# An encoder layer on one Trainium2 core: plain units behind each change of norm, with the new forms made in two stages, and half of the output projection without the seven-product scheme

## The chip, the cores and the metric

The kernel runs on one core of one Trainium2 chip. The metric is the device time of one execution in microseconds (us). Engines are named as in the profile: PE (TensorE, matrix products), DVE (VectorE), ACT (ScalarE), POOL (GpSimd) and SP (SyncE, which here only issues loads). Each engine works through its own queue in program order.

## The reference

One layer of a bidirectional encoder on 256 tokens (T = 256) of width D = 2048, in fp32:

```python
h = h + 1/2 * SwiGLU_1(RMSNorm(h))            # d_ff 5632
u = RMSNorm(h); z = u @ W_in                  # NA q|k|v, MLA q-latent, kv-latent, rope key, gate_A, gate_B
A  = NeighbourhoodAttention2D(q, k, v) @ W_branch_A
Bm = MLA(q-latent, kv-latent, rope key) @ W_branch_B
h = h + (sigmoid(gate_A) * A + sigmoid(gate_B) * Bm) @ W_out
h = h + 1/2 * SwiGLU_2(RMSNorm(h))
h = h + sigmoid(RMSNorm(h) @ W_pl_gate) * (p @ W_pl)
out = RMSNorm(h)
```

The norm is taken four times over the residual stream `h`. Three times matrix products follow at once: ahead of `W_in` (called "mix" in the code), ahead of the second feed-forward ("ffn2"), and ahead of `W_pl_gate` ("pl"). These are the three changes of norm.

## The kernel before

**Products.** An fp32 operand is held as two parts: `hi`, a cast on ACT (L90), and `lo`, a subtraction on DVE (L91). A product of two operands takes three matmuls, `hi*lo`, `hi*hi` and `lo*hi` (L95, L96, L97; `triple`). Weights come from HBM in raw pieces R, of which three are held, and are converted into W pieces by one ACT cast and one DVE subtraction each. An activation operand in this hi/lo layout, transposed so that features lie on partitions, is called a *form*. It covers 256 features (two chunks `kt` of 128); eight forms, 0 to 7, cover `h`. They are written into places X, H or O.

**Units and Blocks.** A `Unit` multiplies by 512 columns of a weight. It consists of granules (class `Granule`); one granule is two chunks of K, one load of 512 KB, one cast, one subtraction of 128x1024, and 12 matmuls for both halves of the tokens, in two PSUM banks. With K = 2048 a unit has 8 granules, 96 matmuls. A `Block` takes 1024 columns jointly over the same K. Of its eight chunk pairs, numbers 2, 4 and 6 (`SEVEN`) are done with 7 products of 2x2 blocks in place of 8; they come in two steps, SevenA and SevenB (9 and 12 matmuls). The other five are `Plain` steps (24 matmuls). So a Block takes 183 matmuls where two units take 192. It needs, of weights and of activations, sums of blocks: a weight chunk takes the DVE operations L259, L261, L262 and two L91 beside it, and its form holds eight tiles, four as they are and four sums. A unit needs the first four only. A Block uses all eight PSUM banks; at its end DVE puts the eight results together, L192 to L195 in `early` and L201 to L204 in the first half of `late`, and then `done` is called.

**Order.** The program is one list of steps (`grans`), in the order in which units and Blocks are made. At each step the next weights are converted ahead (`convert`), as many as there are free W pieces: a granule takes one of four, a Block's step two of six. Then the step's matmuls are issued, and then what `at(d, fn)` has put down for this step. At the last step of a Block (`e.end`) it is otherwise: its matmuls come first, with L192 to L195 and L201 to L204, and only then the next conversions and the rest of `done`.

**Changes of norm.** The last two Blocks ahead of a norm each end in `added`: four residual adds into `h` (L535), and then `new_forms` one and two steps later, which transposes the new columns of `h` on PE (L372), scales them by the norm's gain (L390, L393, L403) and, for forms 2, 4 and 6, builds the four sums (L362) in one scratch piece Z before all eight tiles are split (L90, L91). The squares for the norm follow at five and six steps (L468). The factor `rstd` is not in the forms; it is applied to the products. Behind ffn1 the next thing is the Block of the two latents, behind `W_out` the first Block of ffn2, behind ffn2 the Block of two quarters of `W_pl_gate`. Only ahead of the first feed-forward are there two plain units with forms made in two stages (`first_form`: four tiles; `more_form`: the sums).

**Between.** In the mixing part the latents' Block is followed by one unit of q (NA), the rope key (`kr`: 64 columns, one granule with all 16 chunks), the `W_ukv` and `W_uq` units, three more units of NA q and k; beside these and the Blocks of v the attention runs in small steps put down with `at`. Then come the branches, the gates, and `W_out` as two Blocks.

Of the kernel before, what the change touches and what calls it, by code (L numbers as in the profile page):

```python
# [27 lines left out]
def encoder_kernel(ctx, tc, x, p, ffn1_norm, ffn1_w_gate, ffn1_w_up, ffn1_w_down, mix_norm, w_in,  # L28
# [24 lines left out]
    MPLACE = [("X4", 0), ("X4", 1), ("X6", 0), ("H1", 0), ("X7", 0), ("H1", 1), ("H2", 0), ("H4", 0)]  # L53
    APART = ["H2", "W4", "W5", "H3"]

    def piece(tag, shape, dt=F32):
# [43 lines left out]
    class Unit:  # L100
        def __init__(self, src, K, N, xop, evac, by_token=False, xtile=None):
            self.src, self.K, self.N, self.xop, self.evac, self.by_token = src, K, N, xop, evac, by_token
            self.xtile = xtile or (lambda kt, t: tuple(a[:, t * P:t * P + P] for a in xop(kt)))
            self.per = 1024 // N
            self.load = 2 * self.per if N == 512 else self.per
            self.raw = self.ps = None
            self.kept = []
            self.early = not grans
            if self.early:
                self.load = 2  # L110
            for k0 in range(0, K, self.per):
                grans.append(Granule(self, k0, min(self.per, K - k0)))
# [275 lines left out]
    def scaled(o, ps, gc):  # L388
        if gc is None:
            S.copy(o, ps)  # L390
            return
        for k in range(2):
            S.activation(o[:, k * T:k * T + T], ps[:, k * T:k * T + T], AF.Copy, scale=gT[:, gc + k:gc + k + 1])  # L393
# [31 lines left out]
        at(1, flush)  # L425
        return f

    def new_forms(n, gname, full):
        for i in sorted((2 * n, 2 * n + 1), key=lambda i: i in SEVEN):
            forms[i] = make_form(XPLACE, i, i, h_tile, gcol[gname] + 2 * i, full)  # L430

    zs = []

    def first_form(i):
        ps = plain_tiles(h_tile, i)
        f = forms[i] = place(XPLACE, i)
        if i not in SEVEN:
            plain_form(f, ps, 2 * i)
            return
        if not zs:  # L440
            zs.append(piece("Z", [P, 4, 4, P]))
        z = zs[0][:, i // 2]
        scaled(z.rearrange("p a b -> p (a b)"), ps, 2 * i)
        split(f[:, 0, 0:4], f[:, 1, 0:4], z)

    def more_form(i):
        e = tmp.tile([P, 4, P], F32, tag="pt", name=nm("e"))
        sums(zs[0][:, i // 2], e)
        at(1, lambda: split(forms[i][:, 0, 4:8], forms[i][:, 1, 4:8], e))

    def first_tile(kt, t):
        f = forms[kt // 2]
        n = ((1, 0), (2, 3))[kt % 2][t]
        return f[:, 0, n, :], f[:, 1, n, :]

# [70 lines left out]
    def tmps(tag):  # L526
        return [tmp.tile([P, 512], F32, tag=tag, name=nm(tag)) for _ in range(2)]

    def added(n, nxt, full=True):

        def done(c11, c12, c21, c22):
            for k, t, o in ((n, 0, c11), (n, 1, c21), (n + 1, 0, c12), (n + 1, 1, c22)):
                hs = h[:, t, k * 512:k * 512 + 512]
                if nxt:
                    V.tensor_tensor(out=hs, in0=hs, in1=o, op=ALU.add)  # L535
                else:
                    G.dma_start(hs, o, accum_op=ALU.add)  # L537
            if nxt:
                for k in range(2):
                    at(1 + k, lambda k=k: new_forms(n + k, nxt, full))  # L540
                    next_stat(nxt, n + k, 5 + k)
        return done


# [55 lines left out]
    def mixer():  # L600
# [40 lines left out]
            V.tensor_tensor(out=dst[:, :, 32:64], in0=dst[:, :, 32:64], in1=w2, op=ALU.add)  # L641

        def kr_evac(ps):
            krT = tmp.tile([64, T], F32, tag="s", name=nm("krT"))
            V.tensor_copy(krT, ps[0][0:64, 0:T])

            def tr1():
                r = rstd["mix"]
                b = bank()
                for t in range(2):  # L650
                    PE.transpose(b[:, t * 64:t * 64 + 64], krT[:, t * P:t * P + P], ident[0:64, 0:64])
                kr = []
                for t in range(2):
                    z = tmp.tile([P, 1, 64], F32, tag="s", name=nm("krz"))
                    V.tensor_scalar(out=z[:, 0, :], in0=b[:, t * 64:t * 64 + 64], scalar1=r[:, t:t + 1], scalar2=None,
                                    op0=ALU.mult)
                    o = tmp.tile([P, 2, 64], F32, tag="pt", name=nm("kro"))
                    w = small([P, 2, 32], tag="krw")
                    rope(o[:, 0:1, :], z, t, 1, w[:, 0:1, :], w[:, 1:2, :])
                    V.tensor_copy(o[:, 1, :], o[:, 0, :])  # L660
                    kr.append(o)

                def tr2():
                    hold()
# [29 lines left out]
        def uq_evac(u):  # L694
            def f(ps):
# [5 lines left out]
                if u == 2:  # L701
# [93 lines left out]
        def mla_attention(d0):  # L795
# [28 lines left out]
            for pair in range(4):  # L824
                run(pair, d0 + 4 * pair)

            at(d0 + 17, loose)

        def na_qk_evac(which, u, place):
            def f(ps):  # L830
# [29 lines left out]
        def na_attention(d0):  # L860
# [21 lines left out]
            at(d0 + 17, end)  # L882

            def run(pair, d):
                holder = {}
# [19 lines left out]
                def rest():  # L905
                    B, C = pv_steps(heads, holder, lambda hd, kt: M["nv"][:, kt, hd * P:hd * P + P], None, True)
                    B()
                    at(1, C)
                at(d + 3, rest)
            for pair in range(4):  # L910
                run(pair, d0 + 4 * pair)

# [40 lines left out]
        def ya_evac(n):  # L953
            def f(ps):
                a = tmps("t")
                for t in range(2):
                    V.tensor_tensor(out=a[t], in0=ps[t], in1=M["sga", n, t], op=ALU.mult)
                for t in range(2):
                    V.tensor_tensor(out=a[t], in0=a[t], in1=M["yb"][t][:, n * 512:n * 512 + 512], op=ALU.add)

                def tr():
                    for j in sorted((0, 1), key=lambda j: 2 * n + j in SEVEN):
                        mixed[2 * n + j] = make_form(MPLACE, 2 * n + j, j, lambda t, kt: a[t][:, kt * P:kt * P + P],
                                                     scratch="X0")
                at(1, tr)
            return f

        def oop(key):
            def f(kt):
                o = M[key]  # L970
                return o[0][:, kt, :], o[1][:, kt, :]
            return f

        wi = w_in[0]
# [5 lines left out]
        def plain(c0, evac):  # L980
            unit(rows(wi, c0), 16, 512, None, evac, xtile=first_tile)

        joint(wi, 3584, 3072, x, latents)
        plain(0, na_qk_evac("nq", 0, "H1"))
        unit(rows(wi, 4096, 64), 16, 64, narrow_x, kr_evac)
        for u in range(4):
            unit(rows(w_ukv[0], u * 512), 4, 512, lop("kva"), ukv_evac(u))
# [12 lines left out]
            joint(wi, 4160 + n * 512, 4160 + n * 512 + 512, x, ga_done(n))  # L1000
        for n in range(4):
            unit(rows(w_branch_a[0], n * 512), 8, 512, oop("oa"), ya_evac(n))
        for n in (0, 2):
            joint(w_out[0], n * 512, n * 512 + 512, form_of(mixed), added(n, "ffn2", False))


    def embedding():
# [34 lines left out]
        def pl_evac(n):  # L1042
            def f(ps):
# [13 lines left out]
                def gain():  # L1057
                    for t in range(2):
                        gained(n, t)
                    if n == 2:  # L1060
# [64 lines left out]
    first_pl = len(grans)  # L1125
    E = embedding()
    tasks.setdefault(first_pl, []).append(E["start"])
    tasks.setdefault(first_pl + 1, []).append(lambda: at(1, E["ptr"]))
# [110 lines left out]
```

## Time and profile before

| | |
|---|---|
| runs | 2180.14, 2182.2, 2182.46 us; median 2182.2 us |
| the profiled execution | 2180.34 us, of which the span of the profile is 2178.6 us |
| matmuls and transposes on PE | 9621 |
| busy: PE, DVE, ACT, POOL | 2132.2, 1857.8, 1175.9, 46.5 us |
| HBM | 409.83 MB read, 189 GB/s over the span |

How to read it: times are us from the start of the span. A line of instructions names the engine, the line of the code and `out<-in` in the program's names, with the shape in partitions x elements. In square brackets stands the idle time ahead of an instruction and what ended it. In windows, the columns are the length, the busy time of the engine (with its instructions), the granted clock of PE as a share of full speed, the busy share of the DMA engines and their GB/s.

### The profile page before, as it was taken

To read this page: it belongs to the slowest core of one execution; us is meant where nothing else is said; L and a number is where in the kernel's file an instruction comes from. 1 tells how busy PE (TensorE), PEld (TensorE's weight loads), DVE (VectorE), ACT (ScalarE), POOL (GpSimd) and SP (SyncE) were. 2 spreads that over 40 slices of the span, in tenths; PEclk is the share of its full clock that TensorE was granted. 3 is DMA by queue.
4 is the path that set the end of the run, shared out by engine and by line. 5 is a ranking of instruction groups with operands and counts; after the bars stand their busy time and mean duration, and the time that the engine had idled before them with its cause. 6 is when DMAs were issued, how large, how long until landed. Compare 5 with 4: busy or idle time off the path is not lost.

```text
span 2178.6 us, 25574 instructions
## 1 busy us (share of the span) xinstructions
PE 2132.2 (98%) x9621; PEld 1762.7 (81%) x9621; DVE 1857.8 (85%) x2005; ACT 1175.9 (54%) x1178; POOL 46.5 (2%) x70
## 2 busy tenths in 40 slices
PE   9999999999999899999999999899999999999987
PEld 8888888888887688888888887788888888888766
DVE  6899889998999875576688789899989998899986
ACT  7455455555556545454555555555555555555554
POOL 1000100000000000001000000000000000000000
PEclk9999999999999999999999999999999999999999
DMA  7555866667665455356556555566676657756643
GB/s 261 185 193 195 242 204 207 198 213 220 202 207 176 148 175 172 119 195 193 170 176 210 189 191 163 171 203 202 213 217 207 207 189 226 232 175 202 208 155 135
DMA packets 219052, 422.00 MB, mean 194 GB/s; under 512 B 14600, under 2 KB 15184, under 8 KB 218800
## 3 DMA queue, kind: packets, MB, share of 16 engines
q1 hardware_dynamic: 213072, 408.47, 56.7%
q0 software_dynamic: 5824, 11.89, 3.1%
q8 instruction: 75, 1.23, 0.2%
q14 instruction: 49, 0.40, 0.0%
q10 hardware_dynamic: 32, 0.01, 0.0%
HBM read 409.83 MB, written 2.10 MB: 189 GB/s over the span
## 4 chain that ended last, share of the span: by engine, by line
PE 91%; DVE 4%; ACT 2%; issue 2%; DMA 1%; DVEq 0%; ACTq 0%; POOL 0%; POOLq 0%
PE B L97 29%; PE B L95 29%; PE B L96 29%; DVE W L91 2%; PE B L372 2%; ACT W L90 1%; DMA R<-in_w_branch_b_dram 1%; PE B L783 1%; PE B L769 0%; PE B L811 0%; PE B L810 0%; DVE X L91 0%; ACT sq L468 0%; PE B L894 0%; ACT Z L393 0%
## 5 line engine op out<-in xcount | busy, mean ns | idle before, releaser
L90 ACT CAST W<-R 128x1024 fp32r<-128x1024 f32 (+2 forms) x681 | 936.8, 1382 | 674.3 <-DVE R L259 365.3
L91 DVE TENSOR_TENSOR W<-R,W 128x1024 fp32r<-128x1024 f32 (+2 forms) x681 | 1094.5, 1629 | 211.9 <-ACT W L90 210.3
L95 PE MATMUL B<-W,X 128*128 128x512 f32 x2019 | 796.8, 395 | 16.9 <-DVE H L337 7.6
L97 PE MATMUL B<-W,X 128*128 128x512 f32 x2019 | 789.8, 391 | 6.5 <-DVE W L91 6.5
L96 PE MATMUL B<-W,X 128*128 128x512 f32 x2019 | 788.2, 390 | 0.0
L95 PEld LDWEIGHTS B<-W,X 128*128 128x128 f32 x2019 | 380.8, 189 | 98.7 <-DVE H L337 8.0
L97 PEld LDWEIGHTS B<-W,X 128*128 128x128 f32 x2019 | 380.6, 189 | 88.9 <-DVE W L91 9.1
L96 PEld LDWEIGHTS B<-W,X 128*128 128x128 f32 x2019 | 381.0, 189 | 77.5
L97 PE MATMUL B<-W,H 128*128 128x512 f32 x934 | 364.5, 390 | 6.0 <-DVE W L91 5.7
L95 PE MATMUL B<-W,H 128*128 128x512 f32 x934 | 366.2, 392 | 0.0
L96 PE MATMUL B<-W,H 128*128 128x512 f32 x934 | 363.5, 389 | 0.0
L97 PEld LDWEIGHTS B<-W,H 128*128 128x128 f32 x934 | 175.3, 188 | 45.4 <-DVE W L91 9.0
L96 PEld LDWEIGHTS B<-W,H 128*128 128x128 f32 x934 | 175.4, 188 | 36.0
L95 PEld LDWEIGHTS B<-W,H 128*128 128x128 f32 x934 | 175.4, 188 | 35.7
L259 DVE TENSOR_TENSOR R<-R 128x1024 f32<-128x1024 f32 x119 | 145.8, 1225 | 4.1
L262 DVE TENSOR_TENSOR R<-R 128x512 f32<-128x512 f32 x119 | 82.4, 693 | 4.0
L261 DVE TENSOR_TENSOR R<-R 128x512 f32<-128x512 f32 x119 | 82.4, 692 | 4.1
L390 ACT CAST H<-B 128x512 fp32r<-128x512 f32 x31 | 17.7, 588 | 96.9 <-PE B L372 96.9
L562 ACT ACTIVATE s<-t,sm 128x512 f32<-128x512 f32 x42 | 28.1, 716 | 30.1 <-DVE t L201 30.1
L537 POOL DMA_DIRECT2D h<-t x16 | 13.9, 998 | 1361.8 <-DVE t L201 1143.1
L393 ACT ACTIVATE X<-B,gT 128x256 fp32r<-128x256 f32 x40 | 16.5, 472 | 36.2 <-PE B L372 36.2
L193 DVE TENSOR_TENSOR t<-B,pt 128x512 f32<-128x512 f32 x41 | 28.4, 692 | 1.4
(229 smaller groups left out, 974.4 us busy)
## 6 DMA issues: line engine op xcount, KB each, us to landing
R<-in_ffn_w_down_dram SPq DMA_DIRECT2D x176, 512.0 KB, 5.2
R<-in_ffn_w_gate_dram SPq DMA_DIRECT2D x170, 512.0 KB, 3.8
R<-in_ffn_w_up_dram SPq DMA_DIRECT2D x168, 512.0 KB, 4.8
R<-in_w_in_dram SPq DMA_DIRECT2D x81, 512.0 KB, 4.6
R<-in_w_in_dram SPq DMA_DIRECT2D x24, 1024.0 KB, 5.2
R<-in_w_out_dram SPq DMA_DIRECT2D x32, 512.0 KB, 5.0
R<-in_w_branch_b_dram SPq DMA_DIRECT2D x8, 1024.0 KB, 7.1
R<-in_w_branch_a_dram SPq DMA_DIRECT2D x8, 1024.0 KB, 5.0
```

Of the source, the lines that this page charges most:

```text
L90: S.copy(hi, r)
L91: V.tensor_tensor(out=lo, in0=r, in1=hi.bitcast(F32), op=ALU.subtract)
L95: PE.matmul(o, xl, hi, start=start, stop=False)
L96: PE.matmul(o, xh, hi, start=False, stop=False)
L97: PE.matmul(o, xh, lo, start=False, stop=stop)
L193: V.tensor_tensor(out=self.v, in0=q[7], in1=self.w, op=ALU.add)
L259: V.tensor_tensor(out=raw[:, 0:4:3, :], in0=raw[:, 0:3:2, :], in1=raw[:, 3:4, :].to_broadcast([P, 2, 512]), op=ALU.add)
L261: V.tensor_tensor(out=raw[:, 2, :], in0=raw[:, 0, :], in1=raw[:, 2, :], op=ALU.add)
L262: V.tensor_tensor(out=raw[:, 1, :], in0=raw[:, 2, :], in1=raw[:, 1, :], op=ALU.add)
L372: PE.transpose(ps[:, j * P:j * P + P], src(t, 2 * i + k), ident)
L562: S.activation(s[t], g, AF.Silu, scale=r[:, t:t + 1])
L783: PE.matmul(b[:, j * T:j * T + T], vsl(heads[j], kt), pts[j][:, kt, :], start=(kt == 0), stop=(kt == 1))
```

## The change

It has these parts.

1. **Plain units behind the norms.** Behind ffn1 the first unit of NA q now stands ahead of the latents' Block. Behind ffn2 one unit of `W_pl_gate` and its `W_pl` unit stand ahead of the gates' Block. The second half of `W_out` is two plain units; the first half stays a Block.
2. **Forms in two stages.** For "mix" and "pl", `added` now makes four tiles per form one and two steps later (`first_form`), and the sums of forms 2, 4 and 6 at four, six and eight steps (`more_form`). The scratch Z holds all three forms' tiles at once. The squares move to (4, 7) steps behind the first down Block and (3, 5) behind the second.
3. **W_out.** The Block ends in `wout_done` (residual, forms at +1 and +2, squares at +3 and +4). A plain unit ends in `wout_evac`: the two residual adds read PSUM themselves, and `new_forms` follows at +1.
4. **At a Block's end** the first granule of a unit that follows is now converted ahead of the Block's last matmuls, L192 to L195 and L201 to L204 (`convert(True)`).
5. **Smaller parts.** `kr` is two granules with loads of half the size. One step of the NA attention (`rest`) comes a step later, and the steps that depend on counts are shifted by one. `MPLACE` (the places of the forms of `W_out`) has other entries. The tasks of the last part are counted and placed anew.

```diff
-            self.per = 1024 // N
+            self.per = min(1024 // N, 8)
...
+    def first_form(i, gc=0):
         ps = plain_tiles(h_tile, i)
         f = forms[i] = place(XPLACE, i)
         if i not in SEVEN:
-            plain_form(f, ps, 2 * i)
+            plain_form(f, ps, gc + 2 * i)
             return
-        if not zs:
+        if len(zs) % 3 == 0:
             zs.append(piece("Z", [P, 4, 4, P]))
-        z = zs[0][:, i // 2]
-        scaled(z.rearrange("p a b -> p (a b)"), ps, 2 * i)
+        else:
+            zs.append(zs[-1])
+        z = zs[-1][:, i // 2]
+        scaled(z.rearrange("p a b -> p (a b)"), ps, gc + 2 * i)
         split(f[:, 0, 0:4], f[:, 1, 0:4], z)
...
-            if nxt:
-                for k in range(2):
-                    at(1 + k, lambda k=k: new_forms(n + k, nxt, full))
-                    next_stat(nxt, n + k, 5 + k)
+            for k in range(2):
+                for j in range(2):
+                    at(1 + k, lambda i=2 * (n + k) + j: first_form(i, gcol[nxt]))
+                next_stat(nxt, n + k, (4, 7)[k] if n == 0 else 3 + 2 * k)
+            if n == 2:
+                for j, i in enumerate(sorted(SEVEN)):
+                    at(4 + 2 * j, lambda i=i: more_form(i))
...
-                at(d + 3, rest)
+                at(d + 4, rest)
...
+        def wout_done(*c):
+            for k, t, o in four(0, *c):
+                residual(k, t, o)
+            for k in range(2):
+                at(1 + k, lambda k=k: new_forms(k, "ffn2"))
+                next_stat("ffn2", k, 3 + k)
+
+        def wout_evac(n):
+            def f(ps):
+                for t in range(2):
+                    residual(n, t, ps[t])
+                at(1, lambda: new_forms(n, "ffn2"))
+                next_stat("ffn2", n, 2 if n == 2 else 4)
+            return f
...
+        plain(0, na_qk_evac("nq", 0, "H1"))
         joint(wi, 3584, 3072, x, latents)
-        plain(0, na_qk_evac("nq", 0, "H1"))
...
-        for n in (0, 2):
-            joint(w_out[0], n * 512, n * 512 + 512, form_of(mixed), added(n, "ffn2", False))
+        joint(w_out[0], 0, 512, form_of(mixed), wout_done)
+        for n in (2, 3):
+            unit(rows(w_out[0], n * 512), 16, 512, None, wout_evac(n), xtile=lambda kt, t: plain_tile(mixed, kt, t))
...
+        unit(rows(wg, 1024), 16, 512, None, gate_evac(2), xtile=first_tile)
+        unit(rows(wp, 1024), 2, 512, pop, pl_evac(2))
         Block([rows(wg, 0), rows(wg, 512)], form_of(forms), 8, gates)
-        unit(rows(wp, 0), 2, 512, pop, pl_evac(0))
-        unit(rows(wp, 512), 2, 512, pop, pl_evac(1))
-        unit(rows(wg, 1024), 16, 512, None, gate_evac(2), xtile=first_tile)
+        for n in range(2):
+            unit(rows(wp, n * 512), 2, 512, pop, pl_evac(n))
         unit(rows(wp, 1536), 2, 512, pop, last_pl_evac)
-        unit(rows(wp, 1024), 2, 512, pop, pl_evac(2))
         unit(rows(wg, 1536), 16, 512, None, last_gate_evac, by_token=True, xtile=first_tile)
...
-    def convert():
+    def convert(one=False):
...
-            if step[0] < 0:
+            if one or step[0] < 0:
                 return
...
+        elif ends and todo[0] < len(grans) and isinstance(grans[todo[0]], Granule):
+            convert(True)
```

Three places in the order of DVE show what moves. The names: W are weight pieces (the L91 writes `lo`), R raw pieces, B PSUM banks, t and pt the results of a Block, h the residual stream, X forms, Z the scratch.

The first place is DVE behind the last four L20x of ffn1's last Block, before:

```order
L91 TENSOR_TENSOR W_816_5379<-R_814_5375,W_815_5378 128x2048
L535 TENSOR_TENSOR h<-h,t_5362 128x512
L535 TENSOR_TENSOR h<-h,t_5363 128x512
L535 TENSOR_TENSOR h<-h,pt_5364 128x512
L535 TENSOR_TENSOR h<-h,pt_5365 128x512
L91 TENSOR_TENSOR W_819_5390<-R_817_5386,W_818_5389 128x1536
L259 TENSOR_TENSOR R_817_5386<-R_817_5386 128x2x512
L261 TENSOR_TENSOR R_817_5386<-R_817_5386 128x512
L262 TENSOR_TENSOR R_817_5386<-R_817_5386 128x512
L403 SCALAR_TENSOR_TENSOR X_782_5202<-B_824_5424,gT,X_782_5202 128x256 x2
L362 TENSOR_TENSOR Z_5439<-Z_5439 128x128 x4
L91 TENSOR_TENSOR W_829_5447<-R_817_5386,W_828_5446 128x2x512
```

The same place with the change:

```order
L537 TENSOR_TENSOR h<-h,t_5359 128x512
L537 TENSOR_TENSOR h<-h,t_5360 128x512
L537 TENSOR_TENSOR h<-h,pt_5361 128x512
L537 TENSOR_TENSOR h<-h,pt_5362 128x512
L91 TENSOR_TENSOR W_815_5378<-R_814_5376,W_815_5378 128x1024
L91 TENSOR_TENSOR W_816_5381<-R_814_5376,W_816_5381 128x1024
L91 TENSOR_TENSOR X_820_5403<-Z_5203,X_820_5403 128x512
L403 SCALAR_TENSOR_TENSOR X_785_5213<-B_821_5408,gT,X_785_5213 128x256 x2
L91 TENSOR_TENSOR W_823_5419<-R_822_5417,W_823_5419 128x1024
L91 TENSOR_TENSOR X_825_5439<-Z_5203,X_825_5439 128x512
L403 SCALAR_TENSOR_TENSOR X_827_5449<-B_826_5444,gT,X_827_5449 128x256 x2
L91 TENSOR_TENSOR W_828_5454<-R_822_5417,W_828_5454 128x1024
```

The residual adds stand ahead of the next conversions, these are single granules in place of Block steps with their sums, and the splits of forms have half the elements.

The second place is DVE at the end of the last Block of ffn2. Before:

```order
L91 TENSOR_TENSOR W_2380_15133<-R_2378_15129,W_2379_15132 128x2048
L91 TENSOR_TENSOR W_2385_15153<-R_2383_15149,W_2384_15152 128x2048
L192 TENSOR_TENSOR pt_15194<-B_2371_15090,t_15192 128x512
L193 TENSOR_TENSOR t_15193<-B_2370_15083,pt_15194 128x512
L194 TENSOR_TENSOR pt_15195<-B_2369_15079,t_15193 128x512
L195 TENSOR_TENSOR pt_15194<-B_2369_15079,pt_15194 128x512
L201 TENSOR_TENSOR t_15192<-B_2348_14950,t_15192 128x512
L202 TENSOR_TENSOR t_15193<-B_2349_14957,t_15193 128x512
L203 TENSOR_TENSOR pt_15195<-B_2350_14964,pt_15195 128x512
L204 TENSOR_TENSOR pt_15194<-B_2351_14971,pt_15194 128x512
L91 TENSOR_TENSOR W_2392_15209<-R_2390_15205,W_2391_15208 128x2048
L535 TENSOR_TENSOR h<-h,t_15192 128x512
```

With the change:

```order
L91 TENSOR_TENSOR W_2371_15128<-R_2370_15126,W_2371_15128 128x1024
L91 TENSOR_TENSOR W_2372_15131<-R_2370_15126,W_2372_15131 128x1024
L91 TENSOR_TENSOR W_2376_15152<-R_2375_15150,W_2376_15152 128x1024
L192 TENSOR_TENSOR pt_15181<-B_2360_15071,t_15179 128x512
L193 TENSOR_TENSOR t_15180<-B_2359_15064,pt_15181 128x512
L194 TENSOR_TENSOR pt_15182<-B_2358_15060,t_15180 128x512
L195 TENSOR_TENSOR pt_15181<-B_2358_15060,pt_15181 128x512
L201 TENSOR_TENSOR t_15179<-B_2337_14935,t_15179 128x512
L202 TENSOR_TENSOR t_15180<-B_2338_14942,t_15180 128x512
L203 TENSOR_TENSOR pt_15182<-B_2339_14949,pt_15182 128x512
L204 TENSOR_TENSOR pt_15181<-B_2340_14956,pt_15181 128x512
L91 TENSOR_TENSOR W_2381_15192<-R_2375_15150,W_2381_15192 128x1024
```

Three conversions of granules stand ahead of L192, and a fourth between L204 and the residual adds, which follow it.

The third place is DVE where the last Block of gate_A ends and the units of `W_branch_A` begin. Before:

```order
L91 TENSOR_TENSOR W_1421_8947<-R_1419_8943,W_1420_8946 128x2048
L192 TENSOR_TENSOR pt_8997<-B_1408_8841,t_8995 128x512
L193 TENSOR_TENSOR t_8996<-B_1407_8834,pt_8997 128x512
L194 TENSOR_TENSOR pt_8998<-B_1406_8830,t_8996 128x512
L195 TENSOR_TENSOR pt_8997<-B_1406_8830,pt_8997 128x512
L201 TENSOR_TENSOR t_8995<-B_1393_8745,t_8995 128x512
L202 TENSOR_TENSOR t_8996<-B_1394_8752,t_8996 128x512
L203 TENSOR_TENSOR pt_8998<-B_1395_8759,pt_8998 128x512
L204 TENSOR_TENSOR pt_8997<-B_1396_8766,pt_8997 128x512
L91 TENSOR_TENSOR W_1427_9010<-R_1426_9008,W_1427_9010 128x1024
L91 TENSOR_TENSOR W_1428_9013<-R_1426_9008,W_1428_9013 128x1024
```

With the change:

```order
L91 TENSOR_TENSOR W_1424_8959<-R_1422_8955,W_1423_8958 128x2048
L91 TENSOR_TENSOR W_1426_8985<-R_1425_8983,W_1426_8985 128x1024
L192 TENSOR_TENSOR pt_9014<-B_1411_8853,t_9012 128x512
L193 TENSOR_TENSOR t_9013<-B_1410_8846,pt_9014 128x512
L194 TENSOR_TENSOR pt_9015<-B_1409_8842,t_9013 128x512
L195 TENSOR_TENSOR pt_9014<-B_1409_8842,pt_9014 128x512
L201 TENSOR_TENSOR t_9012<-B_1396_8757,t_9012 128x512
L202 TENSOR_TENSOR t_9013<-B_1397_8764,t_9013 128x512
L203 TENSOR_TENSOR pt_9015<-B_1398_8771,pt_9015 128x512
L204 TENSOR_TENSOR pt_9014<-B_1399_8778,pt_9014 128x512
L91 TENSOR_TENSOR W_1431_9025<-R_1425_8983,W_1431_9025 128x1024
```

The first granule of the unit (`W_1426`) is converted ahead of L192 instead of behind L204.

More of the change, by code (lines that the diff above doesn't have):

```diff
@@ L51, in encoder_kernel @@
     HPLACE = [("H0", 0), ("H0", 1), ("H1", 0), ("H4", 0), ("H2", 0), ("H4", 1), ("H3", 0), ("H5", 0)]
-    MPLACE = [("X4", 0), ("X4", 1), ("X6", 0), ("H1", 0), ("X7", 0), ("H1", 1), ("H2", 0), ("H4", 0)]
+    MPLACE = [("X6", 0), ("X6", 1), ("H2", 0), ("H1", 0), ("X7", 0), ("H1", 1), ("H3", 0), ("H4", 0)]
     APART = ["H2", "W4", "W5", "H3"]
@@ L426, in make_form, with new_forms @@
         return f
-    def new_forms(n, gname, full):
+    def new_forms(n, gname):
         for i in sorted((2 * n, 2 * n + 1), key=lambda i: i in SEVEN):
-            forms[i] = make_form(XPLACE, i, i, h_tile, gcol[gname] + 2 * i, full)
+            forms[i] = make_form(XPLACE, i, i, h_tile, gcol[gname] + 2 * i)
     zs = []
-    def first_form(i):
+    def first_form(i, gc=0):
         ps = plain_tiles(h_tile, i)
@@ L447, in more_form, with plain_tile @@
         e = tmp.tile([P, 4, P], F32, tag="pt", name=nm("e"))
-        sums(zs[0][:, i // 2], e)
+        sums(zs[-1][:, i // 2], e)
         at(1, lambda: split(forms[i][:, 0, 4:8], forms[i][:, 1, 4:8], e))
     def first_tile(kt, t):
-        f = forms[kt // 2]
+        return plain_tile(forms, kt, t)
+    def plain_tile(table, kt, t):
+        f = table[kt // 2]
         n = ((1, 0), (2, 3))[kt % 2][t]
@@ L527, in tmps, with residual, added @@
         return [tmp.tile([P, 512], F32, tag=tag, name=nm(tag)) for _ in range(2)]
-    def added(n, nxt, full=True):
+    def residual(k, t, o):
+        hs = h[:, t, k * 512:k * 512 + 512]
+        V.tensor_tensor(out=hs, in0=hs, in1=o, op=ALU.add)
+    def added(n, nxt):
         def done(c11, c12, c21, c22):
             for k, t, o in ((n, 0, c11), (n, 1, c21), (n + 1, 0, c12), (n + 1, 1, c22)):
-                hs = h[:, t, k * 512:k * 512 + 512]
                 if nxt:
-                    V.tensor_tensor(out=hs, in0=hs, in1=o, op=ALU.add)
+                    residual(k, t, o)
                 else:
+                    hs = h[:, t, k * 512:k * 512 + 512]
                     G.dma_start(hs, o, accum_op=ALU.add)
-            if nxt:
-                for k in range(2):
-                    at(1 + k, lambda k=k: new_forms(n + k, nxt, full))
-                    next_stat(nxt, n + k, 5 + k)
+            if not nxt:
+                return
+            for k in range(2):
[5 more added lines that the diff above has]
+                    at(4 + 2 * j, lambda i=i: more_form(i))
         return done
@@ L643, in kr_evac @@
         def kr_evac(ps):
-            krT = tmp.tile([64, T], F32, tag="s", name=nm("krT"))
+            krT = tmp.tile([64, T], F32, tag="t", name=nm("krT"))
             V.tensor_copy(krT, ps[0][0:64, 0:T])
@@ L734, in f @@
                     at(4, rt)
-                    mla_attention(6)
+                    mla_attention(5)
             return f
@@ L825, in mla_attention @@
                 run(pair, d0 + 4 * pair)
-            at(d0 + 17, loose)
+            at(d0 + 18, loose)
         def na_qk_evac(which, u, place):
@@ L881, in end @@
                 split(*M["oa"], M["nq"])
-            at(d0 + 17, end)
+            at(d0 + 18, end)
             def run(pair, d):
@@ L963, in tr @@
                         mixed[2 * n + j] = make_form(MPLACE, 2 * n + j, j, lambda t, kt: a[t][:, kt * P:kt * P + P],
-                                                     scratch="X0")
+                                                     full=True, scratch="X0")
                 at(1, tr)
@@ L972, in oop @@
             return f
+        def wout_done(*c):
+            for k, t, o in four(0, *c):
+                residual(k, t, o)
+            for k in range(2):
[8 more added lines that the diff above has]
+            return f
         wi = w_in[0]
@@ L1059, in gain @@
                         gained(n, t)
-                    if n == 2:
+                    E["n"] = E.get("n", 0) + 1
+                    if E["n"] == 3:
                         s3 = small([P, 2])
@@ L1127, in encoder_kernel @@
     tasks.setdefault(first_pl, []).append(E["start"])
-    tasks.setdefault(first_pl + 1, []).append(lambda: at(1, E["ptr"]))
+    tasks.setdefault(first_pl + 4, []).append(E["ptr"])
     todo = [0]
-    def convert():
+    def convert(one=False):
         while todo[0] < len(grans):
```

## The prediction, as it was put on record

> **What bounds the kernel now.** I read the page first, then the waits of PE by stretch, then windows over those stretches. The page:
>
> ```profile
> span 2178.6 us, 25574 instructions
> PE 2132.2 (98%) x9621; PEld 1762.7 (81%) x9621; DVE 1857.8 (85%) x2005; ACT 1175.9 (54%) x1178; POOL 46.5 (2%) x70
> ```
>
> PE is busy for 98% of the span, so the end is set by PE: by how many matmuls there are, and by the little that it loses. The time can fall only by what PE loses. The waits of PE (line, what it waited for, sum, times, longest) lie in four stretches: ffn1 to the mixing part (686 to 774), W_out to ffn2 (1300 to 1400), ffn2 to the last part (2032 to 2120), and the whole mixing part between (776 to 1300):
>
> ```profile
> PE B L97 <- DVE W L91: 3.9, 3, 1.6
> PE B L95 <- ACT W L90: 3.0, 1, 3.0
> PE B L353 <- DVE t L623: 2.0, 1, 2.0
> PE B L95 <- DVE t L201: 1.1, 1, 1.1
> PE B L95 <- ACT Z L393: 0.4, 1, 0.4
> ```
>
> ```profile
> PE B L97 <- DVE W L91: 4.0, 3, 1.6
> PE B L95 <- ACT W L90: 2.9, 1, 2.9
> PE B L95 <- DVE t L201: 0.3, 1, 0.3
> PE B L95 <- ACT Z L393: 0.2, 1, 0.2
> ```
>
> ```profile
> PE B L95 <- DVE H L337: 7.6, 1, 7.6
> PE B L97 <- DVE W L91: 2.3, 2, 1.4
> PE B L95 <- DVE t L201: 1.1, 1, 1.1
> PE B L1022 <- issue: 0.5, 1, 0.5
> PE B L95 <- DVE t L1047: 0.3, 1, 0.3
> ```
>
> ```profile
> PE B L769 <- DVE P L756: 2.1, 2, 1.2
> PE B L97 <- DVE W L91: 1.5, 1, 1.5
> ```
>
> The first three lists sum to 10.4, 7.4 and 11.8 us, 29.6 together; the fourth to 3.6. PE waits in the three changes of norm and hardly anywhere else. To see all that is lost there, windows: first a quiet stretch of ffn1, then the three changes and the last unit, counting only the matmuls that read weights:
>
> ```profile
> 470.00:550.00 80.00, 80.00 (x355) 1.00 0.79 236
> 686.11:773.40 87.29, 73.80 (x302) 0.96 0.48 159
> 1311.40:1398.92 87.52, 78.14 (x320) 0.96 0.53 173
> 2032.00:2118.43 86.43, 72.20 (x303) 0.96 0.51 174
> 2118.43:2140.33 21.90, 21.90 (x96) 1.00 0.59 196
> ```
>
> Where nothing waits a matmul takes 80.00/355 = 0.225 to 21.90/96 = 0.228 us; I take 0.2265. At that pace the three changes need 68.4, 72.5 and 68.6 us, and took 18.9, 15.0 and 17.8 more. Transposes are part of that; all PE instructions of the same windows are
>
> ```profile
> 686.11:773.40 87.29, 76.76 (x334) 0.96 0.48 159
> 1311.40:1398.92 87.52, 80.03 (x344) 0.96 0.53 173
> 2032.00:2118.43 86.43, 74.47 (x331) 0.96 0.51 174
> ```
>
> so 32, 24 and 28 others, which add 2.96, 1.89 and 2.27 us of busy time: 0.08 to 0.09 each, where they are not overlapped more. At 0.13 (a choice, to allow for the change of kind at both ends) they come to 4.2, 3.1 and 3.6. What is lost is then 14.7 + 11.9 + 14.2 = **40.8 us**. Named waits make 29.6 of it; part of the rest is the clock:
>
> ```profile
> 738.30:743.10 4.80, 4.79 (x11) 0.50 0.67 218
> 1368.71:1374.80 6.09, 6.09 (x14) 0.50 0.53 172
> 2081.91:2084.60 2.69, 2.69 (x6) 0.50 0.74 202
> ```
>
> Behind the longest wait of each change 31 matmuls ran at a granted clock of 0.50 and so took twice as long; half of 13.6 is 6.8 us. 4.4 stay unnamed (small gaps). With the 3.6 of the mixing part the kernel loses 44.4 us that are neither matmul nor transpose.
>
> Why they wait: the queues of ACT and DVE, behind ffn1 and ffn2.
>
> ```profile
> 731.10 0.84 ACT L393 ACTIVATE Z<-B,gT 128x256 f32<-128x256 f32 x2 [2.33 <-DVE X L91]
> ...
> 2078.96 2.29 DVE L91 TENSOR_TENSOR W<-R,W 128x2048 fp32r<-128x2048 f32 x1 [0.57 <-ACT W L90]
> 2081.17 0.68 DVE L337 TENSOR_TENSOR H<-B,H 128x512 fp32r<-128x512 f32 x1
> ```
>
> ACT stood 2.33 us until DVE had read the one scratch Z, with the casts of weights queued behind it; that is the 3.0 and, with DVE's part, the 1.6 behind it. At ffn2's end a PSUM bank was held until L337, which stood in DVE's queue behind the conversions: the 7.6.
>
> **The change, part by part.** Prices of DVE, from its groups between 660 and 780:
>
> ```profile
> L91 DVE TENSOR_TENSOR W<-R,W 128x2048 fp32r<-128x2048 f32 x11 | 25.1, 2289 | 7.5 <-ACT W L90 7.5
> L91 DVE TENSOR_TENSOR W<-R,W 128x1024 fp32r<-128x1024 f32 x18 | 21.5, 1219 | 0.0
> L403 DVE SCALAR_TENSOR_TENSOR X<-B,gT,X 128x256 fp32r<-128x256 f32 x10 | 4.3, 475 | 0.0
> L91 DVE TENSOR_TENSOR X<-Z,X 128x1024 fp32r<-128x1024 f32 x3 | 3.7, 1220 | 1.2 <-ACT X L90 1.2
> L362 DVE TENSOR_TENSOR Z<-Z 128x128 f32<-128x128 f32 x12 | 2.9, 286 | 1.1 <-ACT Z L393 1.0
> L535 DVE TENSOR_TENSOR h<-h,t 128x512 f32<-128x512 f32 x4 | 2.6, 684 | 0.0
> ```
>
> *Matmuls.* Two units instead of a Block in W_out: 192 - 183 = 9 more, 9 x 0.2265 = **+2.0 us**. Everything else is moved only; kr's products are the same in number.
>
> *Behind ffn1.* The unit that now follows has granules of 12 matmuls, 2.72 us, and asks DVE for 1.22 each; a Block's Plain step asks 2.29 of 5.44, and its SevenA and SevenB far more. The rest of DVE's work in that unit: four residual adds 2.7, four L403 1.9, two splits of four tiles (half of 1.22) 1.2, three sums of four L362 3.4, three splits of sums 1.8; 11.1 us, 1.4 per granule. With 1.22 that is 2.6 of 2.72: it fits, barely, and what is a little late is made up in the Block behind. With three scratch tiles at once, ACT no longer waits for Z as a whole, and a cast of a form has half the elements. Of the 14.7 I leave: one late SevenB conversion of the Block before, whose scale and cast of Z still stand ahead of a weight's cast, 0.9 (0 to the 3.0 seen now); the first transposes, which wait for two residual adds: behind the last matmul come one to four L20x (as L535, 0.68 each) and two adds, 2.0 to 4.1, less one granule of 2.72, so 0 to 1.4, taken as 0.6; and the latents' transposes (L353), which waited 2.0 for L623 and now have one granule of kr ahead of them, about half of its work, 24 small matmuls at half the width, 2.7 us at most: 0.6 taken (0 to 2.0). Left: 2.1.
>
> *Behind W_out.* The sums are gone from the half that is late: the new forms 0 to 3 are made beside 16 granules, and DVE has 16 x 1.5 = 24 us over for them. Forms 4 and 5 follow within the second unit, 6 and 7 behind it, when the first steps of ffn2 read the early forms. The named waits of 7.4 and the clock go; left 0, at worst one cast (3.0).
>
> *Behind ffn2.* The 7.6 goes, since the transposes of p (L1022) and L337 come later, and in a unit, which leaves four banks free. Left: the same 0.9 (0 to 3.0); the transposes. Here DVE has three conversions ahead of L192, against two behind ffn1, and one more between L204 and the adds: two more of 1.22, so 0.6 + 2.4 = 3.0 (0, where DVE's lead covers them, to 3.8). And the last granules, whose order I can't follow to the end, 0.7 (0 to 2.0). Left: 4.6.
>
> A wait of 3.0 stands just where the clock decides: behind 3.0 and 2.9 (and a second one of 1.6 right after), and behind 7.6, it fell to 0.50, and it did not behind the single waits of 1.5 and 2.0. At 0.50 up to 14 matmuls cost 3.0 more; I take none, and keep the 3.0 for the range. [...]
>
> *At a Block's end.* One row carries this, DVE where the Block of gate_A ends:
>
> ```profile
> 1209.95 3.66 DVE L91 TENSOR_TENSOR W<-R,W 128x1024 fp32r<-128x1024 f32 x3
> ```
>
> The first granule of `W_branch_A` was converted only here, behind L204, and PE waited 1.5. Ahead of L192 it is done a Block's step earlier: -1.5 (0 if L192 to L204 are now what PE waits for, since the unit's banks are freed by them; DVE has them 1.22 later, and that is what stands queued behind it).
>
> *NA attention.* PE waited twice for P (2.1 in all). `rest` a step later gives DVE one granule, 2.7 us, against a longest wait of 1.2: both gone. The attention ends a step later, and W4 and W5 come free at the same step as the next Block asks: nothing, or one conversion (2.3).
>
> *Smaller parts.* kr's two loads replace one and come through the same queue with three raw pieces held ahead: nothing, or one load's landing if that lead is gone, 2 to 4 us by the loads in the page's list. POOL and HBM are not near a limit (2%, 189 GB/s). Of the 4.4 unnamed I leave 1.6 (0 to 4.4).
>
> *Sum.* Lost now 44.4. Left 2.1 + 0 + 4.6 + 1.6 = 8.3. So -44.4 + 8.3 + 2.0 = -34.1, against the profiled execution's 2180.3 (span 2178.6 and 1.7 around it): 2146.2. The median of the runs is 1.9 above the profiled one, so between 2146 and 2148: **2147 us**. All lower ends: -44.4 + 2.0 + 0 = -42.4, 2138 to 2140. All upper ends at once, of the three changes (3.0 + 1.4 + 2.0, 3.0, and 3.0 + 3.8 + 3.0 + 2.0) and the unnamed (4.4), are 25.6, so -16.8, 2163.5 to 2165.4.
>
> **Rivals.**
> - *B, half comes back.* The waits move into the new units: the transposes wait for residual adds at each of the three places, the clock halves behind each, and the last unit's granules come late. For it: 1.4 of 1.5 us per granule is no margin, and order in a queue, not the load, made today's waits. Against: DVE's idle time ahead of L91 was 7.5 us in the stretch behind ffn1, so that it isn't full. Half of 44.4 back: -22.2 + 2.0, 2160 to 2162.
> - *C, slower.* DVE becomes the bound of the plain units. It decides once DVE's other work per granule passes 2.72 - 1.22 = 1.5 us; I have 1.4 behind ffn1. If each of the 33 granules (8 + 16 + 8 and the `W_pl` one) came one conversion late, 33 x 1.22 = 40 us: 2146 + 40, about 2187. Against: in W_out there is nearly nothing else for DVE, so that half of the 33 have no cause to wait.
> - *D, no effect.* The order of waits changes, and PE loses the same, because the total of DVE's work is what it was (85% busy). 2178 to 2184. Against: DVE's work falls in the stretches concerned, by the sums' and weights' operations (L259, L261, L262) that move out or go.
>
> **How the numbers follow.** A 0.74, B 0.17, C 0.05, D 0.04. The time predicted is A's. The range runs from A's lower end to B and A's upper end, 2139 to 2164; C, D and the tails of A and B are left out. 0.2%, some 4.4 us, is about what a measurement of this kernel can tell from no change. A and B are faster, 0.91; of D 0.03 lie within that and 0.01 above it: same 0.03, and slower 0.06 with C.
>
> **What would show it.** In the profile after: windows of 87 us behind each norm with 2 to 5 us lost instead of 12 to 15; a granted clock of 1.00 behind ffn1 and W_out; no PE wait for Z (L393) nor for L337 of 7.6; L769 without its wait; the first transposes (L372) of the last change waiting about 3. It is wrong if PE waits for `DVE W L91` in each granule of the new units (C), if L372 waits over 3 at each place with the clock at 0.50 behind it (B), or if the span falls by under 15.

## The result, and the profile after the change

The changed kernel takes 2149.1 us (median of 4 runs, 2146.87 to 2149.42), the kernel before 2182.25 us (4 runs, 2180.14 to 2182.46): a ratio of 0.9848, 95% interval 0.9831 to 0.9865. The forecast was 2147, with 2139 to 2164. The two profiled executions took 2149.42 and 2180.34 us, their spans differ by 30.9.

The page of the kernel after, its first two lines, and then all waits of PE over the whole span:

```profile
span 2147.7 us, 25568 instructions
...
PE 2125.3 (99%) x9630; PEld 1762.0 (82%) x9630; DVE 1841.7 (86%) x1997; ACT 1171.4 (55%) x1186; POOL 46.5 (2%) x70
```

```profile
PE B L372 <- DVE h L537: 3.3, 1, 3.3
PE B L95 <- DVE t L1079: 3.1, 2, 1.9
PE B L97 <- DVE W L91: 2.3, 4, 0.8
PE B L1185 <- POOL ident L293: 1.4, 1, 1.4
PE B L686 <- DVE kro L676: 0.9, 1, 0.9
```

PE has nine matmuls more, as it should. Five lines are left of the waits; L1185 stands at the very start, L686 in the mixing part, and both long ones, L372 and L1079, lie behind ffn2. The windows around the first and the second change of norm say the same; length, busy time, instructions and clock, of before first:

```profile
680.00:780.00 100.00, 89.47 (x398) 0.97 0.48 158
...
1290.00:1400.00 110.00, 102.51 (x447) 0.97 0.55 179
```

Of the kernel after:

```profile
680.00:780.00 100.00, 99.23 (x466) 1.00 0.55 179
1290.00:1400.00 110.00, 109.81 (x497) 1.00 0.57 193
```

PE's idle time went from 10.5 to 0.8 us and from 7.5 to 0.2, and the clock is at 1.00 in both.

To get each part's share, count in both traces the matmuls that read weights (those of L95 to L97 and of `kr`), and compare when the n-th of them starts. Up to the second half of W_out both have the same number for the same work, so a difference in time is time won. From there the kernel after has nine more; the n-th is still compared with the n-th, and the cost of the nine is taken off in the last row.

| up to matmul | before, us | after, us | won so far | won in this part | forecast |
|---|---|---|---|---|---|
| 2801, late in ffn1 | 657.09 | 657.02 | 0.07 | 0.1 | 0 |
| 4001, behind the first norm | 978.15 | 965.22 | 12.93 | 12.9 | 14.7 - 2.1 = 12.6 |
| 4801, behind most of the attention | 1179.91 | 1164.39 | 15.51 | 2.6 | 2.1 |
| 5201, behind branch_a | 1276.01 | 1258.72 | 17.29 | 1.8 | 1.5 |
| 6001, in ffn2 | 1475.63 | 1445.99 | 29.64 | 12.3 | 11.9 |
| last (8907th, 8916th) | | | 31.2 | 3.6, less 2.0 for nine matmuls | 14.2 - 4.6 = 9.6, less 2.0 |

Everything but the last change of norm came as forecast, or a little better; the unnamed small losses, of which 1.6 were to stay, are within these parts. Behind ffn2 6 us less was won.

What is lost there shows at the end of ffn2's last Block, first in a cast on ACT, then in DVE (start, length, and in brackets the wait ahead):

```profile
2024.01 1.05 ACT L90 CAST W<-R 128x1024 fp32r<-128x1024 f32 x1 [1.30 <-DMA R<-in_w_pl_gate_dram]
```

```profile
2025.09 1.23 DVE L91 TENSOR_TENSOR W<-R,W 128x1024 fp32r<-128x1024 f32 x1 [1.01 <-ACT W L90]
2026.23 0.68 DVE L192 TENSOR_TENSOR pt<-B,t 128x512 f32<-128x512 f32 x1
...
2030.68 0.68 DVE L204 TENSOR_TENSOR pt<-B,pt 128x512 f32<-128x512 f32 x1
2031.28 1.22 DVE L91 TENSOR_TENSOR W<-R,W 128x1024 fp32r<-128x1024 f32 x1
2032.41 1.28 DVE L537 TENSOR_TENSOR h<-h,t 128x512 f32<-128x512 f32 x2
```

and in PE's row for the transposes with the window behind it:

```profile
2033.75 1.09 PE L372 MATMUL B<-ident,h 128*128 128x128 f32 x8 [3.26 <-DVE h L537]
...
2033.75:2038.79 5.04, 5.04 (x19) 0.66 0.29 101
```

The third conversion waits 1.0 for its cast, which itself waited 1.30 for the load of its weights; L192 follows only then, so this 1.0 is the load's and not the queue's work. A fourth conversion stands between L204 and the adds, for which PE waits 3.26. Behind that the clock is 0.66 over 5 us. The other wait is near the end:

```profile
2102.78 1.34 ACT L1060 ACTIVATE t<-t,sm 128x512 f32<-128x512 f32 x2 [4.06 <-DVE t L201]
2104.57 1.34 ACT L1060 ACTIVATE pt<-pt,sm 128x512 f32<-128x512 f32 x2 [0.46 <-DVE pt L204]
2105.82 3.87 ACT L90 CAST W<-R 128x1024 fp32r<-128x1024 f32 x4
```

```profile
2106.89 2.36 DVE L91 TENSOR_TENSOR W<-R,W 128x1024 fp32r<-128x1024 f32 x2 [2.34 <-ACT W L90]
2109.16 1.28 DVE L1079 TENSOR_TENSOR t<-B,t 128x512 f32<-128x512 f32 x2
```

```profile
2109.99 0.52 PE L95 MATMUL B<-W,H 128*128 128x512 f32 x1 [1.89 <-DVE t L1079]
2110.31 0.63 PE L96 MATMUL B<-W,H 128*128 128x512 f32 x1
...
2110.20:2114.00 3.80, 3.80 (x11) 0.55 0.93 312
```

Read it upwards: PE wants a PSUM bank that L1079 has to read; L1079 stands behind two conversions in DVE's queue, these behind their casts in ACT's, the casts behind four sigmoids of the gates, and these behind L201 to L204.

### The profile page after: what moved, and what is told of

Same layout as the page of the kernel before. It is cut to its first block, busy times and chain, and to the rows that moved or that the text cites. A ratio compares the mean times of both kernels' runs of the same rounds, so it can differ in the third digit from the quotient of the medians.

```text
span 2147.7 us, 25568 instructions
## 1 busy us (share of the span) xinstructions
PE 2125.3 (99%) x9630; PEld 1762.0 (82%) x9630; DVE 1841.7 (86%) x1997; ACT 1171.4 (55%) x1186; POOL 46.5 (2%) x70
## 4 chain that ended last, share of the span: by engine, by line
PE 95%; DVE 2%; DMA 1%; ACT 1%; issue 1%; DVEq 0%; SPq 0%; ACTq 0%
PE B L97 30%; PE B L95 30%; PE B L96 30%; PE B L372 2%; DVE W L91 1%; DMA H<-in_ffn_w_gate_dram 1%; PE B L799 1%; ACT W L90 0%; PE B L785 0%; PE B L826 0%; PE B L910 0%; PE B L827 0%; DMA R<-in_w_pl_gate_dram 0%; PE B L859 0%; DVE H L345 0%
## 5 line engine op out<-in xcount | busy, mean ns | idle before, releaser
L91 DVE TENSOR_TENSOR W<-R,W 128x1024 fp32r<-128x1024 f32 (+2 forms) x684 | 1088.9, 1616 | 200.8 <-ACT W L90 197.0
L95 PE MATMUL B<-W,X 128*128 128x512 f32 x2006 | 788.3, 393 | 1.4 <-DVE t L1079 1.3
L97 PE MATMUL B<-W,X 128*128 128x512 f32 x2006 | 782.2, 390 | 0.7 <-DVE W L91 0.7
L97 PEld LDWEIGHTS B<-W,X 128*128 128x128 f32 x2006 | 376.8, 188 | 80.8 <-DVE W L91 1.9
L95 PEld LDWEIGHTS B<-W,X 128*128 128x128 f32 x2006 | 377.0, 188 | 79.2 <-DVE t L1079 1.7
L96 PEld LDWEIGHTS B<-W,X 128*128 128x128 f32 x2006 | 377.2, 188 | 77.0
L95 PE MATMUL B<-W,H 128*128 128x512 f32 x950 | 372.9, 392 | 1.9 <-DVE t L1079 1.9
L97 PE MATMUL B<-W,H 128*128 128x512 f32 x950 | 370.8, 390 | 1.5 <-DVE W L91 1.5
L96 PE MATMUL B<-W,H 128*128 128x512 f32 x950 | 370.5, 390 | 0.0
L97 PEld LDWEIGHTS B<-W,H 128*128 128x128 f32 x950 | 178.7, 188 | 39.8 <-DVE W L91 2.5
L95 PEld LDWEIGHTS B<-W,H 128*128 128x128 f32 x950 | 178.8, 188 | 38.8 <-ACT W L90 2.3
L96 PEld LDWEIGHTS B<-W,H 128*128 128x128 f32 x950 | 178.7, 188 | 36.7
L579 DVE SCALAR_TENSOR_TENSOR pt<-pt,sm,s 128x512 f32<-128x512 f32 x42 | 29.6, 745 | 0.0
```

The costliest lines, as they stand in the source:

```text
L91: V.tensor_tensor(out=lo, in0=r, in1=hi.bitcast(F32), op=ALU.subtract)
L95: PE.matmul(o, xl, hi, start=start, stop=False)
L96: PE.matmul(o, xh, hi, start=False, stop=False)
L97: PE.matmul(o, xh, lo, start=False, stop=stop)
L579: V.scalar_tensor_tensor(out=u, in0=u, scalar=rh[:, t:t + 1], in1=s[t], op0=ALU.mult, op1=ALU.mult)
```

## The experiments

The theory: time is lost where DVE's and ACT's queues stand in the wrong order at a change of norm, and is won by units whose granules ask little of them. What was open: which of the parts does it, and why the last change keeps 11 us of loss. All runs start from the changed kernel; the changed one has a ratio of 0.9848 to before.

**Adds first.** At each Block's end with units behind it:

```diff
             more[0]()
-            convert()
-            more[1]()
+            if isinstance(grans[todo[0]], Granule):
+                more[1]()
+                convert()
+            else: ...
```

> Only the order at a Block's end with units behind it is changed: the residual adds of the last Block of ffn2 come ahead of the next granule's conversion. In the profile after the change PE waits 3.3 us there for an add, 11 matmuls behind it run at clock 0.50 (2.2 us). Theory: the adds are late because conversions stand ahead of them in DVE's queue, 1.2 us each; the wait falls to 2.1, the clock stays at 1.00, and the time falls by 3.3 us, to about 2146. Rival 1: the clock falls behind 2.1 us as well, -1.2 us only. Rival 2: the conversion, now behind the adds, is waited for in its turn, 0.

Measured: 2148.98 us, 0.9853 (0.9838 to 0.9867). Behind ffn2 the wait fell to 2.1 and the clock stayed at 1.00 over the next 4.6 us; between the 8201st matmul and the end the kernel is 3.8 us faster than the changed one, 2.8 of it ahead of the first wait for L1079, and 1.0 near the end, where PE waits 1.68 for L1079 and the clock doesn't fall (from the second on, the matmuls behind it take 0.39 to 0.40 us each up to 2119; in the changed kernel they take 0.63 there). But the edit is too wide: at gate_A's end `done` holds sigmoids, which now came ahead of the casts, and 2.4 us were lost there.

```profile
1195.93 1.33 ACT L963 ACTIVATE H<-pt,sm 128x512 f32<-128x512 f32 x2 [0.46 <-DVE pt L204]
1197.18 2.93 ACT L90 CAST W<-R 128x1024 fp32r<-128x1024 f32 x3
```

```profile
1198.26 0.50 PE L95 MATMUL B<-W,H 128*128 128x512 f32 x1 [1.36 <-ACT W L90]
...
2035.36:2040.00 4.64, 4.64 (x29) 1.00 0.27 81
```

The theory holds at its place; what comes first in a queue depends on what `done` does.

**The place alone.** Only at ffn2's end, with no granule converted at that step ahead of L192:

```diff
-        elif ends and todo[0] < len(grans) and isinstance(grans[todo[0]], Granule):
+        elif ends and g != first_pl - 1 and todo[0] < len(grans) and isinstance(grans[todo[0]], Granule):
...
+            if g == first_pl - 1:
+                more[1]()
+                convert()
+            else: ...
```

> At the end of ffn2's last Block alone: no granule is converted ahead of L192 at that step, and the residual adds come ahead of the next conversions (two conversions ahead of L192, none before the adds). Theory (the wait of 3.3 is two conversions of 1.2 and what L192 waited for them, the half clock hangs on its length): the wait falls to 1 us or less, the clock stays at 1.00, -4.5 to -5.5 us, about 2144. Rival (PE waits later for the granules now converted behind the adds): -1 or less.

Measured: 2143.77 us (2143.35 to 2143.82), 0.983 (0.9813 to 0.9846); by the spans 5.6 us less than the changed kernel. By the matmuls' starts 5.0 are won at ffn2's end and 1.0 near the end, where the clock doesn't fall (0.39 to 0.40 us for each matmul from the second behind the wait of 1.71 for L1079); 0.4 were lost before. PE's waits from 2000 us on in this run, all:

```profile
PE B L95 <- DVE t L1079: 3.0, 2, 1.7
PE B L97 <- DVE W L91: 1.4, 2, 0.8
```

L372 doesn't wait any more, and the granules converted later aren't waited for: of the two waits for L91 one stands at 2012.7, inside ffn2's last Block, the other at 2120.2. DVE shows why: L192 comes right behind two conversions, the adds right behind L204.

```profile
2022.12 2.35 DVE L91 TENSOR_TENSOR W<-R,W 128x1024 fp32r<-128x1024 f32 x2
2024.39 0.68 DVE L192 TENSOR_TENSOR pt<-B,t 128x512 f32<-128x512 f32 x1
...
2028.84 0.68 DVE L204 TENSOR_TENSOR pt<-B,pt 128x512 f32<-128x512 f32 x1
2029.43 1.28 DVE L537 TENSOR_TENSOR h<-h,t 128x512 f32<-128x512 f32 x2
```

**The early conversion undone** (`convert(True)` and its condition removed).

> The conversion of the next unit's first granule ahead of a Block's end is undone, all else as changed. It changes DVE's order at three Block ends only (values to branch_b, gate_A to branch_a, ffn2 to the last part). Theory: the 1.6 us wait of the first branch_a granule comes back, branch_b's may come as well, and behind ffn2 the wait of 3.3 gets shorter by 0.7, perhaps with full clock: +0 to +2 in all. Rival: the early conversion does nothing there, and the 1.5 were won by something else: 0 at branch_a.

Measured: 2148.5 us, 0.9852 (0.9838 to 0.9867), so no difference that the runs resolve. By the matmuls' starts it lost 1.8 us at branch_a, where the wait of before is back, and won 3.8 behind ffn2: 2.7 at its end, where L372 waits 2.2 and the clock stays at 1.00 over the next 4.75 us, and 1.1 near the end of the kernel, where it doesn't fall either (0.39 to 0.40 us for each matmul from the second behind the wait of 1.66 for L1079).

```profile
1195.53 0.50 PE L97 MATMUL B<-W,H 128*128 128x512 f32 x1 [1.46 <-DVE W L91]
...
2034.25 1.09 PE L372 MATMUL B<-ident,h 128*128 128x128 f32 x8 [2.18 <-DVE h L537]
```

The part does what the prediction gave it at branch_a, and costs more than that behind ffn2.

**Forms in one stage.** Units where they are, but forms 2, 4 and 6 whole at one and two steps:

```diff
-                for j in range(2):
-                    at(1 + k, lambda i=2 * (n + k) + j: first_form(i, gcol[nxt]))
+                at(1 + k, lambda k=k: new_forms(n + k, nxt, True))
...
-            if n == 2:
-                for j, i in enumerate(sorted(SEVEN)):
-                    at(4 + 2 * j, lambda i=i: more_form(i))
```

> The plain units stay behind the norms, but forms 2, 4, 6 are made whole at one and two steps (sums and all eight tiles) as before the change. Theory (the two stages matter as much as the units): ACT waits for Z again and the splits double, PE loses some 3 to 5 us more behind ffn1 and 2 to 5 behind ffn2, 2154 to 2159. Rival (the units alone do it, since a granule leaves DVE 1.5 us over): within 1 us of 2149.

Measured: 2149.55 us, 0.9855 (0.984 to 0.987): the rival. ACT waits for Z as it did before, but PE's waits between 680 and 780 are small, all of them:

```profile
723.91 0.84 ACT L393 ACTIVATE Z<-B,gT 128x256 f32<-128x256 f32 x2 [2.00 <-DVE X L91]
```

```profile
PE B L97 <- DVE W L91: 0.6, 2, 0.4
PE B L372 <- DVE h L537: 0.5, 1, 0.5
```

By the matmuls' starts two stages win 1.2 us behind ffn1 and lose 0.3 behind ffn2, where with one stage L372 waits longer (3.9) but only one wait for the bank is left. The units, with the squares' new steps, do nearly all.

**W_out as two Blocks again** (the residual by DVE, whole forms, squares at five and six steps):

```diff
-        joint(w_out[0], 0, 512, form_of(mixed), wout_done)
-        for n in (2, 3):
-            unit(rows(w_out[0], n * 512), ...)
+        for n in (0, 2):
+            joint(w_out[0], n * 512, n * 512 + 512, form_of(mixed), wout_done(n))
```

> W_out as two Blocks again, all else as changed (residual by DVE as in the Block half of the change, whole forms at one and two steps, squares at five and six). Theory: the 11.9 us won behind W_out come back and the 9 matmuls (2.0 us) go: +9 to +10 us, about 2158.5. Rival: the waits behind W_out were removed by the adds' place and not by the units, within 2 us of 2147.

Measured: 2152.9 us, 0.987 (0.9855 to 0.9885): only 3.8 us above the changed kernel, where 9 to 10 were expected. By the matmuls' starts 10.9 were lost behind W_out, as the theory has it, with the waits of before, between 1300 and 1400:

```profile
PE B L97 <- DVE W L91: 3.4, 3, 1.3
PE B L95 <- ACT W L90: 2.9, 1, 2.9
PE B L95 <- DVE t L201: 0.3, 1, 0.3
PE B L95 <- ACT Z L393: 0.2, 1, 0.2
```

2.0 came back for nine matmuls, and 5.6 behind ffn2, 700 us later. There the clock doesn't fall behind the wait of 2.1 for the bank near the end (L1080 in this kernel; 0.39 to 0.40 us for each matmul from the second behind it, up to 2119), and the wait for L372 is gone, since nothing stands between L204 and the adds:

```profile
2037.53 0.68 DVE L204 TENSOR_TENSOR pt<-B,pt 128x512 f32<-128x512 f32 x1
2038.12 1.28 DVE L537 TENSOR_TENSOR h<-h,t 128x512 f32<-128x512 f32 x2
```

How many granules are converted ahead depends on which W pieces are free, and that is handed on from unit to unit through all of ffn2. From ffn2 on both kernels have the same code. So the 3.3 at the last change is no price of the new order there, but of the state in which W_out's units leave the pieces. This is worked out from the code; no run starts ffn2 from the other state and keeps W_out's units.

**The attention's step back** (`at(d + 3, rest)`).

> Only the attention's step is put back to three steps from four (its end stays a step later). Theory: the two waits for P (2.1 us, with restarts 2.5) come back, +2.1 to +2.5, about 2151.4. Rival: they were gone by the order of what comes before, 0.

Measured: 2151.73 us (2149.94 to 2153.5), 0.9867 (0.9852 to 0.9882). By the medians the step back costs 2.6 us, about as expected. The trace is that of the slowest of the four runs: the waits for P are back, and by the matmuls' starts they cost 5.0 us in it, since behind the first two the clock fell, to 0.64 over 3.2 us:

```profile
1002.20 0.33 PE L785 MATMUL B<-ident,P 128*128 128x128 f32 x1 [0.28 <-DVE P L772]
1004.06 1.64 PE L785 MATMUL B<-ident,P 128*128 128x128 f32 x7 [1.53 <-DVE P L772]
...
1005.30:1008.50 3.20, 3.20 (x11) 0.64 0.60 162
```

**The tail.** Three runs at the waits for L1079. First the order of the last `W_pl` units, so that the one that is copied out at once comes first.

> Only the order of the last three W_pl units is changed: the one whose result is copied out at once goes first. Theory: the 1.9 us wait for L1079 near the end exists because three short units share two pairs of PSUM banks, and the third needs the banks of the first, whose product needs the sigmoids of the gates; with the copied one first the banks are free: -1.5 to -2.0 us, about 2147.3. Rival: the wait moves unchanged to the last gate unit, which needs the banks of the next: 0.

Measured: 2148.73 us, 0.9853 (0.9837 to 0.987). The rival, in another form: PE waits 1.9 for the copy (L1106), which stands in DVE's queue behind the same conversions. Then other banks (gate 2: 2 and 3; its `W_pl` unit: 0 and 1; the last `W_pl` unit: 4 and 5).

> Only PSUM banks are changed: the unit of gate 2 gets banks 2 and 3, its W_pl unit 0 and 1, the last W_pl unit 4 and 5. Theory: both waits for L1079 (1.3 and 1.9, with restart 1.4 and 2.1) are waits for a bank and go: -3.0 to -3.5 us, about 2146. Rival: behind the bank PE waits for the next granule's conversion, which stands in the same queue: -1 or less.

Measured: 2147.64 us, 0.985 (0.9835 to 0.9864), 1.5 less than the changed kernel and so between the theory and the rival. Both waits for L1079 are gone; behind ffn2 two others stand in their place, one of them for a bank again, since the Block still reads 2 and 3 when the unit begins. L372, which comes right behind, no longer waits. (The lines are two further down in this kernel.)

```profile
PE B L97 <- DVE W L91: 3.4, 4, 1.0
PE B L95 <- DVE pt L206: 2.7, 1, 2.7
```

Last, banks that nobody needs (2 and 6, and 4 and 5), with the repair of ffn2's end:

> The changed kernel with two repairs: the order at ffn2's end of the run pl_adds (which won 5.3 us), and other PSUM banks for two W_pl units, chosen so that nobody waits for them behind ffn2: 2 and 6 for the one ahead of the gates' Block, 4 and 5 for the last. Theory: both waits for L1079 go and no new one comes in their place: 2143.8 - 3.0 = about 2140.5. Rival: as with the banks tried before, PE waits for a conversion instead, 2142 to 2144.

Measured: 2143.5 us (2142.93 to 2143.75), 0.9827 (0.9814 to 0.9841): within 0.3 us of the repair alone. PE's waits from 2000 us on:

```profile
PE B L97 <- DVE W L91: 3.4, 4, 1.0
PE B L97 <- DVE H L91: 0.2, 1, 0.2
```

No bank is waited for, and PE waits 3.4 for conversions instead of 1.4. The bank was what PE waited for, DVE's queue is what makes it late.

**Both repairs, forms in one stage.**

> The same two repairs, but with the forms made whole at one and two steps in place of two stages. Theory after the run one_stage (two stages win nothing by themselves): within 1 us of the kernel with both repairs and two stages. Rival (the two stages' gain was hidden by the waits that are now repaired): 2 us or more slower than it.

Measured: 2143.3 us (2143.0 to 2145.08), 0.9829 (0.9815 to 0.9842): no difference to two stages. These two and the repair alone beat both kernels; the repair of ffn2's end is all that this takes.

No run takes the units behind ffn1 or behind ffn2 away by themselves, and none undoes `kr`, `MPLACE` or the new steps of the squares alone. That the units win the time is shown by an undoing behind W_out; at the other two places it is argued from the run with forms in one stage.

## Why the prediction was right, and where it was off

- *What bounds.* Right: PE's losses at three places were the sum to be won, 40.8 and 3.6 us, and 33.2 of 44.4 were won, against 36.1 forecast. That the total came so near is partly luck: 6.0 too few behind ffn2 are offset by 1.5 more elsewhere and by the 1.6 that were left for small losses.
- *Behind ffn1.* Right in size, 12.9 against 12.6. Wrong in a step: "ACT no longer waits for Z as a whole" was given as a cause. With whole forms ACT waits 2.0 for Z as before and PE hardly notices, since, as far as the order of DVE tells, a granule asks less and later. The transposes and the latents were to keep 1.2; neither waited.
- *Behind W_out.* Right: 12.3 against 11.9, and with two Blocks 10.9 come back. The nine matmuls cost what was said, 2.0.
- *Attention and branch_a.* Right, shown by undoing each: 2.6 (by the medians) and 1.8 won. That the early conversion costs 2.7 at ffn2's end was not seen as its price, although the count of three conversions had it.
- *Smaller parts.* Right that the halved loads of `kr` cost nothing: they landed in 3.0 us (median), and PE waits for no weight there. The loads in the page's list, of 512 and 1024 KB, took 3.8 to 7.1 us, not the 2 to 4 that the prediction reads from it. Not foreseen is a wait of 0.9 for the rotated rope key (L686), which the kernel before doesn't have.
- *Behind ffn2.* The step that was mis-sized: 4.6 were to be left, some 11 were: the late SevenB conversion 0.9 (0.9 forecast), the wait for L372 with its restart (from the start of the matmul ahead of it, less that one's 0.2265 us) 3.4 (3.0), the half clock behind it 1.7 (taken as none, kept for the range), the two waits for L1079 with their restarts 1.4 and 2.0 and the half clock behind the second 1.7 (0.7 for "the last granules"). The order of the last part, which the prediction said it could not follow, held the largest surprise: three short units in a row behind a Block whose sigmoids hold up the casts.
- *Rival B* was right at this one place, not at the others. *C* came nowhere: PE waits for L91 of weights only four times in the whole span, 2.3 us in all. *D* is out.

## What to carry to other kernels

Where an engine is busy for 86% of the span and works through its queue in order, as DVE here, a wait at a change of phase is made by what stands ahead of one instruction, and it is read by following the queue upwards; freeing the resource that the matmul waits for (here a bank) only renamed the wait, since the queue behind it stayed. Work that asks less per step of the busy engines, put behind such a change, hides even an unimproved preparation. And an edit in one phase can move a wait in another through a pool of buffers, so a part undone is read place by place, not by the total.

## What the runs showed of the hardware

The half clock doesn't follow the length of a wait alone. In the changed kernel the clock fell behind waits of 3.26 and 1.89 us (0.66 over the 5.04 us and 0.55 over the 3.80 us of the windows above; matmuls that took 0.39 us took 0.63), and in the run with the attention's step back behind 0.28 and 1.53 with a transpose between (0.64 over 3.20 us). It stayed at 1.00 behind 2.1 (adds first, over 4.64 us), 2.2 (early conversion undone, over 4.75 us) and 2.0 (before, at L353, from 772.05 to 776.00). So the forecast, which took a wait of 3.0 to stand just where the clock decides, set this too high: it fell behind 1.89. What else counts is not shown by these runs.

The cost of each fall in the changed kernel is 1.7 us, an estimate from those windows: 5.04 x (1 - 0.66) and 3.80 x (1 - 0.55). The 1.0 to 1.1 us that three runs win near their end come with a clock that didn't fall there, behind waits of 1.66 to 1.71 for L1079 in place of 1.89.
